# A two-layer hybrid trunk on one core: one product for the second token tile's scores, a reordered mLSTM block loop, one ScalarE table for its gates, and fewer early gate blocks

## The chip, the cores and the metric

The kernel runs on one core of one Trainium2 chip. The metric is the device time of one execution in microseconds (us). A core has five engines with a queue each: TensorE (PE in the profile, with its weight loads listed as PEld), VectorE (DVE), ScalarE (ACT), GpSimd (POOL) and SyncE (SP, which here only starts DMAs).

## The reference

Two layers over 256 tokens of width 1024, all in float32. Layer 0 mixes tokens with a gated MLP, layer 1 with an mLSTM block; after each mixer come a layer norm, a SwiGLU channel mixer, a second layer norm and a sigmoid-gated embedding. What the change touches is mostly the mLSTM mixer:

```python
xm, z = jnp.split(x @ w_in, 2, axis=-1)
xc = jax.nn.silu(causal_depthwise_conv(xm, conv_w, conv_b))
q = headwise_linear(xc, w_q)
k = headwise_linear(xc, w_k)
v = headwise_linear(xm, w_v)
gates = jnp.concatenate([q, k, v], axis=-1) @ w_gates + b_gates
...
s = jnp.einsum('bhtd,bhsd->bhts', qb, kb) * jnp.exp(dmat - m_t[..., None])
...
h = layer_norm(h, norm_g).reshape(B, S, ML_INNER) + skip * xc
return (h * jax.nn.silu(z)) @ w_out
```

and around it, in each layer:

```python
x = layer_norm(ALPHA * x + y, ln1_g[i], ln1_b[i])
x = layer_norm(ALPHA * x + swiglu(x, ffn_w_gate[i], ffn_w_up[i], ffn_w_down[i]), ln2_g[i], ln2_b[i])
gate = jax.nn.sigmoid(x @ ple_w_gate[i] + ple_b_gate[i])
x = x + gate * (p[i] @ ple_w_proj[i])
```

The chunk is 128 tokens, so the 256 tokens are two token tiles, and the gate recurrence is computed over the whole sequence at once.

## The kernel before, in words

**Numbers in two parts.** Every float32 operand of a product is split into a high part (a cast, on ScalarE) and a low part (the difference, on VectorE); the helper is `split` (L152 to L154). A product of two operands is then three products on TensorE: high by high, high by low, low by high. All these casts and subtractions carry L154 in the profile; the tile's name tells them apart (`w` for weights).

**Weights.** All weights arrive as 128 x 1024 blocks (512 KB) in one order, `weight_plan` (L76). `ahead(loads, casts)` (L171) starts loads up to `LOAD_AHEAD` blocks beyond the one in use and splits up to `casts` of them (usually four). A loaded block waits in one of four `raw` buffers; a buffer comes free when VectorE has written the block's low part, and SP then starts the next load. `EARLY` (L51) moves single blocks of the next stage forward in the order, behind named blocks: "mo" is the mLSTM output projection (16 blocks), "g" and "u" are the SwiGLU gate and up projections, "pj" the embedding projection, "pg" its gate, "z" the mLSTM's z projection, "xm" its other input projection. `behind["cast"]` names instructions; the split of a weight traced after that is queued behind them on their engine (L195), without waiting for their result. A layer norm sets it to its own last VectorE instruction (L346).

**The mLSTM block loop** (L799). For each of 16 feature blocks s: `xm_block(s)` (24 products of 256 columns, the causal convolution on VectorE, Silu, the split of xc, the skip term on GpSimd), `qv_block(s-2)` (q and v of an earlier block, with k folded into q, and 8 gate columns added to q and v each), `s_block(s-3)` (the scores). After the blocks named in `Z_AFTER_XM` (L45) comes one z block (24 products).

**The scores** (L777). Tile 0 of the keys meets all 256 tokens and the 8 gate columns: three products of 264 columns. Tile 1 meets only the second 128 tokens and the gate columns: three products of 136 columns. After the fourth block of a head, ScalarE copies scores and gate columns out of PSUM and GpSimd adds the gate columns to `gacc`.

**The gates** (L823 to L887). ScalarE's order there is the written one. z block 8 is multiplied with four transposes of `gacc` in it; then Exp, Ln and two scans on VectorE give the running gate values; z block 9; z block 10 with the transposes of the gate columns at step 3 (`transpose_cols`) and a broadcast of the gates for heads 0 and 1 at step 6; z block 11 with the broadcast for heads 2 and 3; per head three Exp, a product with the scores, a split. z block 12 and one Silu over five z blocks end this part. Then come four `pv_block`s with z blocks 13 to 15 between them.

**The end of the mLSTM and the boundary.** `Down` (L292) multiplies the output projection; for the last four blocks (`HOLD`) the second token tile's products are held back. `boundary` (L507) then runs the layer norm of tile 0 on VectorE while TensorE does the held products and the embedding projection, then the layer norm of tile 1 while TensorE goes on to `first(0)` (L524): for "g" and then for "u", 16 products with the high part of x that walk through the blocks 0 to 3 of the weight, then 8 with the low part. `rsqrt` (L317) is an addition and a power on GpSimd.

Of the kernel before, what the change touches and what calls it, by code (L numbers as in the profile page):

```python
# [11 lines left out]
AF = mybir.ActivationFunctionType  # L12
# [31 lines left out]
TOK = [slice(0, P), slice(P, 2 * P)]  # L44
Z_AFTER_XM = {3: 4, 7: 5, 11: 6, 15: 7}  # L45

# [4 lines left out]
EARLY = {("wo", 17 + k): ("g", 0, k) for k in range(4)}  # L51
EARLY |= {("mo", 6 + 2 * k): ("g", 1, k) for k in range(4)}
EARLY[("mo", 13)] = ("pj", 1, 0)
EARLY |= {("d", l, 10 + k): ("pg", l, k) for l in range(2) for k in range(6)}
# [80 lines left out]
def trunk(ctx, tc, a, out):  # L135
# [181 lines left out]
    def rsqrt(o, var, n=1):  # L317
        ve = tl("c", [P, 2], name="ve")
        pool.tensor_scalar(ve[:, :n], var, EPS, None, ALU.add)  # L319
        pool.tensor_tensor(o, ve[:, :n], mhalf[:, :n], ALU.pow)  # L320
# [177 lines left out]
    def channel_mixer(l, acc, last, hook=None):  # L498
# [8 lines left out]
        def boundary(j, g, b):  # L507

            w = weight("pj", l, j, casts=int(at["use"] <= place["pj", l, j]))
            ln_residual(0, acc.ps[0], g, b)  # L510
            acc.finish()
            project_p(j, w, 0)
            transpose_x(0)
            ln_residual(1, acc.ps[1], g, b)
            project_p(j, w, 1)
# [72 lines left out]
        def gate(t, pieces, before=(None, None)):  # L588
            ps = [bank("A", [P, c.stop - c.start], "gate") for c in pieces]
            if t == 0:  # L590
                gw.extend(None for _ in range(KD))
            for js in [[j] for j in range(len(pieces))] if t else [range(len(pieces))]:
                for i in range(2):
                    for k in range(KD):
                        if t == 0 and i == 0:
                            gw[k] = weight("pg", l, k)
                        if i == 1 and k == before[0]:
                            before[1]()
                        for j in js:
                            mm_part(ps[j], i, t, k, gw[k], pieces[j])  # L600
            return ps
# [20 lines left out]

        p0 = gate(0, HALF, (GATE_STEP, lambda: transpose_x(1)))
        embed(0, HALF, p0)
# [49 lines left out]
    def mlstm(embed1):  # L674
# [55 lines left out]
        def xm_block(f):  # L730
# [11 lines left out]
            for j in (1, 2, 3):  # L742
                dve.scalar_tensor_tensor(y[:, j:], ps[:, :S - j], par[:, f, 3 - j:4 - j], y[:, j:], ALU.mult, ALU.add)
            act.activation(y, y, AF.Silu)
            split(xm[1][:, 0, :], xm[1][:, 1, :], y)
            xms[f] = xm
            pool.tensor_scalar(a1[f // 8][:, f % 8, :], y, par[:, f, 5:6], None, ALU.mult)
# [29 lines left out]
        def s_block(f):  # L777


            h, j = f // 4, f % 4  # L780
            if j == 0:
                pss[:] = [bank("A", [P, S + 8], "s0"), bank("A", [P, GW], "s1")]
            q, k = qs.pop(f), xms.pop(f)[1]
            for s in range(2):
                m = slice(s * P, S + 8)
                pe.matmul(pss[s], k[:, 0, TOK[s]], q[:, 0, m], start=j == 0, stop=False)
                pe.matmul(pss[s], k[:, 0, TOK[s]], q[:, 1, m], start=False, stop=False)
                pe.matmul(pss[s], k[:, 1, TOK[s]], q[:, 0, m], start=False, stop=j == 3)
            if j == 3:
                t = tl("m2", [P, 384], name="sc")  # L790
                g = tl("cf", [P, 2, 8], name="gsum")
                act.copy(g[:, 0], pss[0][:, S:])
                act.copy(t[:, 0:S], pss[0][:, :S])
                act.copy(g[:, 1], pss[1][:, P:])
                act.copy(t[:, S:384], pss[1][:, :P])
                pool.tensor_tensor(gacc, gacc, g, ALU.add)
                sc.append(t)

        for s in range(NI + 3):  # L799
            if s < NI:  # L800
                xm_block(s)
            if s == 1:
# [3 lines left out]
            if 2 <= s < NI + 2:  # L806
                qv_block(s - 2)
            if s >= 3:
                s_block(s - 3)
# [259 lines left out]
```

## Time and profile before

| | us |
|---|---|
| median of 3 runs | 831.73 (830.5 to 832.65) |
| the profiled execution | 831.34 |
| its span, first to last instruction | 829.5 |

The granted TensorE clock was 0.999 of full speed over the span. The profile gives for each engine when each instruction started, how long it took, and what released it where it waited. A matmul's listed duration includes its way through the array; what counts for throughput is the distance from the start of one to the start of the next. In a row of the timeline the first number is the start (us from the start of the span), the second the duration, "x8" a count of merged instructions, and "[0.34 <-POOL q L760]" an idle time of 0.34 us that the named instruction ended.

### The profile page before, as it was taken

What the parts mean: (1) busy time and instruction counts of PE and PEld (TensorE: products, weight loads), DVE (VectorE), ACT (ScalarE), POOL (GpSimd) and SP (SyncE); (2) the same over time, 40 slices, a digit from 0 to 9 for tenths busy, and PEclk for the clock granted to TensorE, in tenths of its full rate; (3) what the DMA queues carried; (4) which work ended last, traced back from release to release, by engine and by line L of the source; (5) the groups of instructions that cost most, each with busy time, mean ns of one, the idle gap of its engine ahead of it and who ended that gap; (6) DMA issues with size and microseconds to landing.
All of it is one profiled execution on the core that took longest, in us unless ns stands there. A gap on an engine that the chain in (4) does not pass through costs nothing.

```text
span 829.5 us, 12434 instructions
## 1 busy us (share of the span) xinstructions
PE 820.4 (99%) x4536; PEld 710.5 (86%) x4536; DVE 615.1 (74%) x967; ACT 476.2 (57%) x825; POOL 157.0 (19%) x215
## 2 busy tenths in 40 slices
PE   9999999999999999999999999999999999999997
PEld 6888888888888888888889999898878888888886
DVE  7757998678945667586878988689885656776674
ACT  7555766566444546475347788776543555665522
POOL 1021633433100000700102766330010000000010
PEclk9999999999999999999999999999999999999999
DMA  8885456568286567586234444361746655776501
GB/s 303 293 310 176 152 171 212 181 202 275 98 282 198 171 208 251 165 289 199 67 135 148 141 142 157 123 237 55 253 139 242 202 179 188 262 242 220 178 1 52
DMA packets 44998, 155.54 MB, mean 188 GB/s; under 512 B 5256, under 2 KB 6024, under 8 KB 44936
## 3 DMA queue, kind: packets, MB, share of 16 engines
q1 hardware_dynamic: 44792, 154.60, 56.5%
q8 instruction: 36, 0.59, 0.3%
q10 hardware_dynamic: 144, 0.13, 0.1%
q14 instruction: 26, 0.21, 0.1%
HBM read 153.67 MB, written 1.05 MB: 187 GB/s over the span
## 4 chain that ended last, share of the span: by engine, by line
PE 83%; DVE 10%; DMA 3%; ACT 2%; POOL 1%; issue 1%; DVEq 0%; ACTq 0%; SPq 0%; POOLq 0%
PE pu L261 8%; PE pg L261 8%; PE acc L241 8%; PE acc L242 8%; PE acc L243 8%; PE ups L261 5%; PE pg L265 4%; PE pu L265 4%; DVE w L154 3%; PE ups L265 3%; PE vps L243 3%; PE vps L241 3%; PE vps L242 3%; PE first L287 2%; PE first L288 2%; PE first L290 2%
## 5 line engine op out<-in xcount | busy, mean ns | idle before, releaser
L154 DVE TENSOR_TENSOR w<-raw,w 128x1024 fp32r<-128x1024 f32 (+1 forms) x279 | 336.2, 1212 | 79.1 <-ACT w L154 77.9
L154 ACT CAST w<-raw 128x1024 fp32r<-128x1024 f32 (+1 forms) x278 | 286.7, 1041 | 129.0 <-PE acc L243 26.1
L241 PE MATMUL acc<-w,h 128*128 128x512 f32 x336 | 131.9, 393 | 0.3 <-ACT w L154 0.3
L243 PE MATMUL acc<-w,h 128*128 128x512 f32 x336 | 131.0, 390 | 1.1 <-DVE w L154 1.1
L242 PE MATMUL acc<-w,h 128*128 128x512 f32 x336 | 131.4, 391 | 0.0
L243 PEld LDWEIGHTS acc<-w,h 128*128 128x128 f32 x336 | 63.1, 188 | 15.5 <-DVE w L154 1.9
L241 PEld LDWEIGHTS acc<-w,h 128*128 128x128 f32 x336 | 63.2, 188 | 12.8 <-ACT w L154 1.1
L242 PEld LDWEIGHTS acc<-w,h 128*128 128x128 f32 x336 | 63.2, 188 | 10.9
L261 PE MATMUL pg<-xs,w 128*128 128x512 f32 x288 | 71.6, 391 | 0.0
L261 PE MATMUL pu<-xs,w 128*128 128x512 f32 x288 | 71.5, 390 | 0.0
L261 PEld LDWEIGHTS pu<-xs,w 128*128 128x128 f32 x288 | 53.8, 188 | 11.1
L261 PEld LDWEIGHTS pg<-xs,w 128*128 128x128 f32 x288 | 53.8, 188 | 11.0
L319 POOL TENSOR_SCALAR ve<-mv 128x1 f32<-128x1 f32 x8 | 6.1, 764 | 294.3 <-DVE mv L339 294.3
L272 ACT COPY s<-pg 128x256 f32<-128x256 f32 x36 | 13.4, 372 | 77.1 <-PE pg L265 77.1
L273 DVE TENSOR_TENSOR s<-s,pg 128x256 f32<-128x256 f32 x36 | 15.1, 420 | 48.8 <-ACT s L272 48.8
L261 PE MATMUL ups<-xs,w 128*128 128x512 f32 x192 | 47.7, 391 | 0.0
L261 PEld LDWEIGHTS ups<-xs,w 128*128 128x128 f32 x192 | 35.7, 188 | 7.2
L265 PEld LDWEIGHTS pg<-xs,w 128*128 128x128 f32 x288 | 38.9, 188 | 3.1
L265 PE MATMUL pg<-xs,w 128*128 128x256 f32 x288 | 39.5, 280 | 0.0
L265 PE MATMUL pu<-xs,w 128*128 128x256 f32 x288 | 39.4, 279 | 0.0
L241 PE MATMUL vps<-w,xs 128*128 128x512 f32 x96 | 37.5, 390 | 0.1
L242 PE MATMUL vps<-w,xs 128*128 128x512 f32 x96 | 37.5, 390 | 0.0
(242 smaller groups left out, 1639.9 us busy)
## 6 DMA issues: line engine op xcount, KB each, us to landing
raw<-in_ffn_g SPq DMA_DIRECT2D x44, 512.0 KB, 4.2
raw<-in_ffn_u SPq DMA_DIRECT2D x44, 512.0 KB, 4.2
raw<-in_ffn_d SPq DMA_DIRECT2D x44, 512.0 KB, 4.4
raw<-in_gm_u SPq DMA_DIRECT2D x24, 512.0 KB, 3.6
raw<-in_gm_wo SPq DMA_DIRECT2D x24, 512.0 KB, 3.5
raw<-in_gm_v SPq DMA_DIRECT2D x21, 512.0 KB, 4.8
raw<-in_ple_gate SPq DMA_DIRECT2D x16, 512.0 KB, 4.4
raw<-in_ml_z SPq DMA_DIRECT2D x16, 512.0 KB, 3.8
```

Of the source, the lines that this page charges most:

```text
L154: return dve.tensor_copy(hi, src) if fast else act.copy(hi, src), sub.tensor_tensor(lo, src, hi.bitcast(F32), ALU.subtract)
L241: pe.matmul(ps, lh, w[:, 0, c], start=start, stop=False)
L242: pe.matmul(ps, ll, w[:, 0, c], start=False, stop=False)
L243: pe.matmul(ps, lh, w[:, 1, c], start=False, stop=stop)
L261: pe.matmul(ps, w[:, 0, k * P:(k + 1) * P], xs[:, k], start=k == 0, stop=False)
L265: pe.matmul(ps[:, 0], w[:, 1, k * P:(k + 1) * P], xh[:, k, :], start=False, stop=k == KD - 1)
L272: act.copy(o, ps[:, 1])
L273: dve.tensor_tensor(o, o, ps[:, 0], ALU.add)
L287: pe.matmul(ps, xh[:, k, TOK[t]], w[:, 0, c], start=k == 0, stop=False)
L288: pe.matmul(ps, xh[:, k, TOK[t]], w[:, 1, c], start=False, stop=False)
L290: pe.matmul(ps, xl[:, k, TOK[t]], w[:, 0, c], start=False, stop=k == KD - 1)
L319: pool.tensor_scalar(ve[:, :n], var, EPS, None, ALU.add)
```

## The change

Seven edits, all in one step:

- `s_block`: for key tile 1, the high part of k meets both parts of q in one product of 2 x 136 columns into two halves of a bank, and the low part of k meets the high part of q in one of 136; the two halves are added on the way out (one ScalarE copy, one VectorE addition, and two GpSimd additions in place of one).
- `xm_block` is cut in two: Silu, the split of xc and the skip term become `xc_block(s)`, traced behind `qv_block(s-2)`.
- z blocks 4, 5, 6 follow blocks 1, 5, 10 in place of 3, 7, 11.
- In the gates' part: one table set with Exp and Ln is loaded ahead; `transpose_cols` stands at step 1 of z block 10, both broadcasts at steps 4 and 7 of it; z block 12 moves behind the first `pv_block`, and each of the four is followed by one z block.
- `EARLY`: three gate blocks (not four) come behind output blocks 8, 10, 12 (not 6, 8, 10, 12), and the embedding projection's first block is not moved any more.
- In the embedding's gate: two blocks (not four) are split ahead, and the next stage's first split is queued behind tile 1's transposes.
- `rsqrt`: the addition moves from GpSimd to VectorE.

```diff
-Z_AFTER_XM = {3: 4, 7: 5, 11: 6, 15: 7}
+Z_AFTER_XM = {1: 4, 5: 5, 10: 6, 15: 7}
...
-EARLY |= {("mo", 6 + 2 * k): ("g", 1, k) for k in range(4)}
-EARLY[("mo", 13)] = ("pj", 1, 0)
+EARLY |= {("mo", 8 + 2 * k): ("g", 1, k) for k in range(3)}
...
-        pool.tensor_scalar(ve[:, :n], var, EPS, None, ALU.add)
+        dve.tensor_scalar(ve[:, :n], var, EPS, None, ALU.add)
...
-            w = weight("pj", l, j, casts=int(at["use"] <= place["pj", l, j]))
+            w = weight("pj", l, j, casts=1)
...
-                            gw[k] = weight("pg", l, k)
+                            gw[k] = weight("pg", l, k, casts=min(2, KD - k))
...
-        p0 = gate(0, HALF, (GATE_STEP, lambda: transpose_x(1)))
+        def second_tile():
+            behind["cast"] = transpose_x(1)
+            ahead(LOAD_AHEAD, 1)
+        p0 = gate(0, HALF, (GATE_STEP, second_tile))
...
+            xms[f] = xm
+            return y
+
+        def xc_block(f, y):
             act.activation(y, y, AF.Silu)
-            split(xm[1][:, 0, :], xm[1][:, 1, :], y)
-            xms[f] = xm
+            split(xms[f][1][:, 0, :], xms[f][1][:, 1, :], y)
             pool.tensor_scalar(a1[f // 8][:, f % 8, :], y, par[:, f, 5:6], None, ALU.mult)
...
-                pss[:] = [bank("A", [P, S + 8], "s0"), bank("A", [P, GW], "s1")]
+                pss[:] = [bank("A", [P, S + 8], "s0"), bank("A", [P, 2, GW], "s1")]
...
-            for s in range(2):
-                m = slice(s * P, S + 8)
-                pe.matmul(pss[s], k[:, 0, TOK[s]], q[:, 0, m], start=j == 0, stop=False)
-                pe.matmul(pss[s], k[:, 0, TOK[s]], q[:, 1, m], start=False, stop=False)
-                pe.matmul(pss[s], k[:, 1, TOK[s]], q[:, 0, m], start=False, stop=j == 3)
+            s0, s1 = pss
+            pe.matmul(s0, k[:, 0, TOK[0]], q[:, 0], start=j == 0, stop=False)
+            pe.matmul(s0, k[:, 0, TOK[0]], q[:, 1], start=False, stop=False)
+            pe.matmul(s0, k[:, 1, TOK[0]], q[:, 0], start=False, stop=j == 3)
+            pe.matmul(s1, k[:, 0, TOK[1]], q[:, :, P:], start=j == 0, stop=False)
+            pe.matmul(s1[:, 0], k[:, 1, TOK[1]], q[:, 0, P:], start=False, stop=j == 3)
...
-                act.copy(g[:, 1], pss[1][:, P:])
-                act.copy(t[:, S:384], pss[1][:, :P])
-                pool.tensor_tensor(gacc, gacc, g, ALU.add)
+                act.copy(t[:, S:], s1[:, 1])
+                dve.tensor_tensor(t[:, S:], t[:, S:], s1[:, 0], ALU.add)
+                pool.tensor_tensor(gacc[:, 0], gacc[:, 0], g, ALU.add)
+                pool.tensor_tensor(gacc[:, 1], gacc[:, 1], t[:, 384:], ALU.add)
...
             if 2 <= s < NI + 2:
                 qv_block(s - 2)
+            if s < NI:
+                xc_block(s, y)
...
+            tc.keep_in_program_order(act.preload_act_table_set("natural_log_exp_and_others"))
...
-            z = z_mm(10, {3: transpose_cols, 6: broadcast_gates})
+            z = z_mm(10, {1: transpose_cols, 4: broadcast_gates, 7: broadcast_gates})
...
-                    z = z_mm(11, {2: broadcast_gates})
+                    z = z_mm(11)
...
-            z_copy(*z_mm(12))
-            act.activation(sz[1][:, 0:5, :], sz[1][:, 0:5, :], AF.Silu)
+            act.activation(sz[1][:, 0:4, :], sz[1][:, 0:4, :], AF.Silu)
...
-            if h < NH - 1:
-                z_act(*z_mm(13 + h))
+            z_act(*z_mm(12 + h))
```

More of the change, by code (lines that the diff above doesn't have):

```diff
@@ L781, in s_block @@
             if j == 0:
-                pss[:] = [bank("A", [P, S + 8], "s0"), bank("A", [P, GW], "s1")]
+                pss[:] = [bank("A", [P, S + 8], "s0"), bank("A", [P, 2, GW], "s1")]
             q, k = qs.pop(f), xms.pop(f)[1]
-            for s in range(2):
-                m = slice(s * P, S + 8)
-                pe.matmul(pss[s], k[:, 0, TOK[s]], q[:, 0, m], start=j == 0, stop=False)
-                pe.matmul(pss[s], k[:, 0, TOK[s]], q[:, 1, m], start=False, stop=False)
-                pe.matmul(pss[s], k[:, 1, TOK[s]], q[:, 0, m], start=False, stop=j == 3)
-            if j == 3:
[L790 to L793, printed above, removed]
-                act.copy(g[:, 1], pss[1][:, P:])
-                act.copy(t[:, S:384], pss[1][:, :P])
-                pool.tensor_tensor(gacc, gacc, g, ALU.add)
-                sc.append(t)
+            s0, s1 = pss
[4 more added lines that the diff above has]
+            pe.matmul(s1[:, 0], k[:, 1, TOK[1]], q[:, 0, P:], start=False, stop=j == 3)
+            if j == 3:
+                t = tl("m2", [P, 384 + 8], name="sc")
+                g = tl("cf", [P, 8], name="gsum")
+                act.copy(g, s0[:, S:])
+                act.copy(t[:, 0:S], s0[:, :S])
+                act.copy(t[:, S:], s1[:, 1])
+                dve.tensor_tensor(t[:, S:], t[:, S:], s1[:, 0], ALU.add)
+                pool.tensor_tensor(gacc[:, 0], gacc[:, 0], g, ALU.add)
+                pool.tensor_tensor(gacc[:, 1], gacc[:, 1], t[:, 384:], ALU.add)
+                sc.append(t[:, :384])
         for s in range(NI + 3):
             if s < NI:
-                xm_block(s)
+                y = xm_block(s)
             if s == 1:
```

## The prediction

> **What bounds the kernel now.** I read the page's first part first, then the busy times of the mLSTM's block loop (a window of 56 us), then TensorE's waits from the start of that loop to the end of the mLSTM.
>
> ```profile
> span 829.5 us, 12434 instructions
> PE 820.4 (99%) x4536; PEld 710.5 (86%) x4536; DVE 615.1 (74%) x967; ACT 476.2 (57%) x825; POOL 157.0 (19%) x215
> ```
>
> ```profile
> 464.00:520.00 56.00, 56.00 (x479) 56.00 (x479) 48.79 (x110) 44.74 (x121) 36.47 (x49) 1.00 0.46 151
> ```
>
> ```profile
> PEld acc L243 <- DVE w L154: 1.9, 2, 1.0
> PEld s L786 <- POOL q L760: 1.1, 2, 0.6
> PEld acc L241 <- ACT w L154: 1.1, 2, 0.8
> PEld vps L768 <- DVE q L154: 0.7, 1, 0.7
> PEld qps L247 <- DVE xm L154: 0.5, 1, 0.5
> PEld cp L850 <- DVE gt L840: 0.4, 1, 0.4
> ```
>
> TensorE is busy 99% of the span, and in the middle of the block loop (464 to 520) it never stands still, while VectorE works 48.79 of 56.00 us there. So an edit is worth what it takes off TensorE's own stream, plus the stalls in this short list that it ends, minus the stalls that it makes. Work taken off another engine is worth nothing by itself. All the stalls that the change can reach lie in five places: the start of the block loop (qps, and one of the two of "s"), its end (vps and the other "s"), the gates (cp), and the last output blocks (acc).
>
> **Part 1: the scores' products.** Here is one block of scores, with the v products ahead of it; what counts is the distance between starts.
>
> ```profile
> 516.42 0.29 PE L768 MATMUL vps<-w,xm 128*128 128x272 f32 x1
> 516.55 0.23 PE L769 MATMUL vps<-w,xm 128*128 128x136 f32 x1
> 516.61 0.34 PE L768 MATMUL vps<-w,xm 128*128 128x272 f32 x1
> ...
> 516.84 0.33 PE L786 MATMUL s<-q,xm 128*128 128x264 f32 x1
> 517.01 0.28 PE L787 MATMUL s<-q,xm 128*128 128x264 f32 x1
> 517.13 0.28 PE L788 MATMUL s<-q,xm 128*128 128x264 f32 x1
> 517.25 0.23 PE L786 MATMUL s<-q,xm 128*128 128x136 f32 x1
> 517.32 0.28 PE L787 MATMUL s<-q,xm 128*128 128x136 f32 x1
> 517.43 0.28 PE L788 MATMUL s<-q,xm 128*128 128x136 f32 x1
> 517.54 0.33 PE L246 MATMUL zps<-xs,w 128*128 128x256 f32 x1
> ```
>
> The six products take 517.54 - 516.84 = 0.70 us. A product of 136 columns holds the stream 0.07 us if a longer one stood before it (517.25 to 517.32), but 0.11 us in a row of short ones (517.32, 517.43, 517.54): then the next weight load isn't done. The pair that the change makes stands in the v products already: 272 columns take 0.13 us, the 136 behind them 0.06. The new block is 0.17 + 0.12 + 0.12 + 0.13 + 0.06 = 0.60 us, 0.10 less; 16 blocks give 1.6 us, all of it on TensorE's stream. The bounds are 0 (columns alone count) and 16 x 0.11 = 1.8 (one product in a row of short ones less).
>
> The Trainium skill, "TensorE: Matmul & The Clock Gate", section "Back-to-back issue gap", speaks against this part: its gap for an isolated product is the columns over 2.4 plus 2.5 ns, so that the same 408 columns for key tile 1 cost the same in two products as in three, but for one 2.5 ns; by it the part saves 16 x 2.5 ns = 0.04 us, an estimate. The rows disagree: 136 columns at 0.11 us are nearly twice that rule's 59 ns. For a stream of weight loads and products the same section gives about 81 ns at 128 columns, which is nearer and still below the rows.
>
> **Part 2: the block loop's stalls.** Four stalls, 0.5 + 0.7 + 1.1 = 2.3 us by weight loads. The qps stall is xc's low part arriving late for the first `qv_block`; z block 4 behind block 1 puts 24 products ahead of it. The other three have one cause: ScalarE, VectorE and GpSimd run in order, and Silu, xc's split and the skip term of block s stand ahead of q's split and the copy of q's gate columns (L760) of block s-2. `xc_block` behind `qv_block` turns that round. What is late next is xc, but it is wanted two blocks later, behind some 48 products. I take -2.3. The bound the other way is below, among the rivals: VectorE is 87% busy, gets four additions more, and z blocks now come after five blocks.
>
> **Part 3: the gates.**
>
> ```profile
> 528.51 1.28 ACT L835 ACT_TABLE_LOAD   x1
> ```
>
> ```profile
> L771 DVE TENSOR_TENSOR vsum<-vsum,vps 128x136 f32<-128x136 f32 x32 | 9.0, 284 | 0.3 <-ACT vsum L770 0.3
> ```
>
> The load in front of Ln stands in the chain from `gacc` to the transposes of the gate columns; without it the chain is 1.28 us shorter. The transposes come two steps earlier, 2 x 3 products of 0.12 us (517.01 to 517.13), 0.7 us. So 0.6 us of slack comes in for a wait of 0.4: -0.4. Against that, tile 1's gate columns now pass through one more VectorE addition (the L771 form, 0.28 us) and one more small GpSimd addition before z block 8's transposes at step 3, while TensorE gets there sooner: +0.3. Moving z block 12 changes no product; it brings the first `pv_block` forward by 24 products (2.8 us), which the shorter chain, the earlier broadcast and the missing table load in front of the third Exp pay back about; I take 0, with 0 to +0.8 as bounds.
>
> **Part 4: the output blocks and the gate blocks.** First what goes. In the last output blocks TensorE waits for splits:
>
> ```profile
> 600.93 0.39 PE L243 MATMUL acc<-w,h 128*128 128x512 f32 x1
> 601.65 0.50 PE L241 MATMUL acc<-w,h 128*128 128x512 f32 x1 [0.33 <-ACT w L154]
> 601.99 0.39 PE L242 MATMUL acc<-w,h 128*128 128x512 f32 x1
> 602.91 0.50 PE L243 MATMUL acc<-w,h 128*128 128x512 f32 x1 [0.53 <-DVE w L154]
> ```
>
> Undisturbed starts are 0.23 us apart (below), so these gaps of 0.72 and 0.92 us lose 0.5 and 0.7; the list above has the second kind twice, 1.9 us in all. Each block passes through one of four raw buffers, and before output block 15 the order held five foreign blocks; now it holds three, and the fourth gate block and the projection's block come after it. Two blocks less are two splits of about 1.2 us less ahead of blocks 14 and 15: -1.9, with 0 as the other bound.
>
> Then what comes. Here is the boundary behind it: VectorE, SP's loads, one ScalarE row, TensorE.
>
> ```profile
> 617.96 0.75 DVE L345 SCALAR_TENSOR_TENSOR xn<-xn,rs,row 128x512 f32<-128x512 f32 x1
> 618.63 4.62 DVE L154 TENSOR_TENSOR w<-raw,w 128x1024 fp32r<-128x1024 f32 x4
> ...
> 626.73 2.48 DVE L154 TENSOR_TENSOR w<-raw,w 128x1024 fp32r<-128x1024 f32 x2 [2.27 <-ACT w L154]
> ```
>
> ```profile
> 598.86 6.73 SPq L177 DMA_DIRECT2D raw<-in_ffn_u  x4
> ...
> 619.88 0.33 SPq L177 DMA_DIRECT2D raw<-in_ffn_g  x1
> ```
>
> ```profile
> 625.64 1.05 ACT L154 CAST w<-raw 128x1024 fp32r<-128x1024 f32 x1 [3.04 <-DMA raw<-in_ffn_g]
> ```
>
> ```profile
> 615.39 0.39 PE L287 MATMUL first<-w,xs 128*128 128x512 f32 x1
> 615.62 0.39 PE L288 MATMUL first<-w,xs 128*128 128x512 f32 x1
> ...
> 621.63 0.47 PE L287 MATMUL first<-w,xs 128*128 128x512 f32 x1
> ```
>
> Before, the four raw buffers hold the four up blocks through the two layer norms, and the four splits start when the second norm ends (L346 puts them behind it). Now the fourth gate block is first in that row, and the fourth up block has no buffer until that split is done. TensorE needs the gate block's low part at its 14th product, 615.39 + 13 x 0.23 = 618.4; the split, a quarter of the 4.62, ends at about 618.63 + 1.2 = 619.8: 1.4 us late. The fourth up block takes the place of the load that SP starts at 619.88, which ScalarE can cast at 625.64 and VectorE has split at 626.73 + 1.24 = 627.97. TensorE wants it at 621.63 + 13 x 0.23 = 624.6: 3.4 us late, which includes the first 1.4. All these times shift together with the end of the output products, so the gap stays. I take +3.4; the bounds are 1.4 (the up block comes in time after all) and 4.6 (one more split of 1.2 us ahead of the layer norm, by the embedding projection's block).
>
> **Part 5: what costs nothing.**
>
> ```profile
> L319 POOL TENSOR_SCALAR ve<-mv 128x1 f32<-128x1 f32 x8 | 6.1, 764 | 294.3 <-DVE mv L339 294.3
> ```
>
> `rsqrt`'s addition leaves GpSimd (0.76 us) for VectorE, in layer norms that run under held products; no wait of TensorE in the list, which covers one of the four boundaries, is on a layer norm. Without that cover it would be worth at most those 0.8 us per norm. Two gate blocks split ahead instead of four, with z's first split behind the transposes, clears ScalarE and VectorE in front of those transposes: a gain of at most a few tenths, taken as 0. ScalarE's missing table loads, other than Ln's, lie in its idle time.
>
> **The sum.** -1.6 - 2.3 - 0.4 + 0.3 - 1.9 + 3.4 = -2.5 us. The sum is made against the profiled execution's 831.34 us (span 829.5, 1.8 around it): 828.8 us. The median of the runs, 831.73, is 0.4 above that execution, well inside their spread. A measurement of this kernel can tell about 0.3%, 2.5 us, from no change, so the forecast stands on the edge of what counts as faster (829.2).
>
> **The rivals.**
> - *The late gate block does not bite* (VectorE gets its split in between the two layer norms, or the up block lands sooner): without +3.4 the sum is -5.9, 825.4 us. For it: layer 0's boundary shows no such stall; against it: there all four gate blocks were early, and L346 orders the splits. 0.22.
> - *The output blocks stay late too*, since their loads, not the number of blocks ahead, are what is slow (ScalarE waits there as well): +1.9, 830.7 us. 0.10.
> - *VectorE becomes the bound of the block loop; slower than before.* The place is blocks 1 to 15. It works 48.79 of 56.00 us; the rest is waiting that doesn't shrink if the order of its work is at fault. It decides as soon as those 7.2 us of idle time can't be cut by the 1.3 us that TensorE would gain there (some 13 blocks at 0.10). Then 1.6 and 2.3 are not gained, and four additions of 0.28 us come on top: +5.0 against the forecast, 833.8 us. For it: z blocks, which give VectorE time, now follow after five blocks; against it: no stall in the 56 us before. 0.08.
> - *No gain from the products*, by columns alone, as the page named in part 1 would have it: 828.8 + 1.6 = 830.4 us. The rows at 517.32 to 517.54 speak against it. 0.04.
> - *The forecast*: 0.52. Other mishaps, new waits in the gates above all: 0.04.
>
> **How the numbers follow.** Within the forecast's case, its unknown ends (1.4 or 4.6 for 3.4, 0.8 in the gates) spread it from about 826.9 to 830.8, a little more than half of it below 829.2: 0.31 faster, 0.21 same. The first rival adds 0.22 to faster; the second, the fourth and half of the third go to same, 0.18; the other half of the third, with most of the mishaps, makes 0.07 slower, and the last 0.01 is same. So 0.53, 0.40 and 0.07. The range reaches from the first rival's 825.4, a little lower for its own spread, to 832.0, which leaves out the third rival and little else.
>
> **What would show it.** Right: 32 products less, and 0.60 us from the first of a scores block to what follows; no wait at qps, vps, "s" or cp; no wait for weights in the output products; then a wait in `first` at the 14th product for the gate block's low part, and a second for the fourth up block, whose load starts only when the second layer norm is over; two ScalarE table loads less. Wrong: `first` runs without a wait (then 825.4), or waits appear inside the block loop on VectorE (then the third rival), or the stalls at blocks 14 and 15 are still there.

## The result, and the profile after

| | before | after |
|---|---|---|
| median of 4 runs each, us | 831.91 (830.5 to 832.65) | 827.16 (826.69 to 827.46) |
| the profiled execution, us | 831.34 | 827.14 |
| its span, us | 829.5 | 825.4 |

The ratio of the times is 0.9943, with a 95% interval of 0.9927 to 0.9959: 4.75 us less. The prediction was 828.8 us, 2.5 less than the profiled execution of before, with a range from a little under 825.4 to 832.0 and "faster" as the likeliest case; the profiled executions differ by 4.2 us, their spans by 4.1. In all that follows, stages are compared within profiled executions, all of which had a granted clock of 0.999 or 1.0; e2 below alone has runs at a lower one (its six longest, 0.994 to 0.997), so that its median says little.

First the page of after: its span, its engines, and the chain that ended last. (Line numbers of after are shifted: `split` is L153, the products are L240 to L247 and L286 to L289, the scores L791 to L796.)

```profile
span 825.4 us, 12401 instructions
...
PE 817.7 (99%) x4520; PEld 708.6 (86%) x4520; DVE 615.5 (75%) x981; ACT 471.4 (57%) x819; POOL 152.3 (18%) x209
...
PE 95%; DVE 2%; DMA 1%; ACT 1%; issue 0%; SPq 0%; POOL 0%; DVEq 0%; ACTq 0%
```

TensorE has 16 products less (4520 for 4536, one in each scores block; the 32 in the prediction's list of signs were a slip) and stays the bound; VectorE's busy time is the same. Then the waits of TensorE's weight loads, from the block loop to the boundary behind the mLSTM (in all, times, longest):

```profile
PEld first L286 <- ACT w L153: 1.6, 1, 1.6
PEld acc L240 <- ACT hn L943: 0.6, 1, 0.6
PEld first L287 <- DVE w L153: 0.3, 1, 0.3
PEld cp L863 <- DVE gt L853: 0.3, 1, 0.3
PEld gp L840 <- POOL sums L804: 0.2, 1, 0.2
PEld num L915 <- POOL plo L153: 0.2, 1, 0.2
PEld qps L245 <- DVE q L153: 0.2, 1, 0.2
```

Of before's list the waits at "s", vps, qps (for `xm`, near the loop's start) and in the output products (acc for `w`) are gone. The qps in this list is another one, for q at the loop's end (519.50). The one at cp is still there, at 0.3 for 0.4, and a new one in `first` is the largest. Small ones have come in the gates (gp, num), and the one in the first output blocks (acc for `hn`) has grown from 0.2 to 0.6.

Where the 4.1 us came from is read off the start of each stage's first product on TensorE. A difference that changes from one row to the next arose between them.

| first product of | before | after | difference |
|---|---|---|---|
| layer 0's first stage | 4.92 | 5.17 | +0.25 |
| layer 0's embedding gate | 405.53 | 406.06 | +0.53 |
| the block loop (xmps) | 441.24 | 441.45 | +0.21 |
| the transposes of `gacc` (gp) | 526.49 | 522.91 | -3.58 |
| the output projection | 563.68 | 560.08 | -3.60 |
| the embedding projection (pps) | 611.78 | 606.03 | -5.75 |
| `first` | 615.39 | 609.65 | -5.74 |
| layer 1's channel mixer (pg) | 638.43 | 634.36 | -4.07 |
| the last product of all | 824.89 | 820.81 | -4.08 |

So the block loop gave 3.79 us (-3.58 less +0.21), the gates 0.02, the output products 2.15, and `first` took back 1.67. The embedding gate of layer 0 gave 0.32. What comes before it was 0.53 later, and all of that arose in the first 72 us, in a stage that the change leaves as it is. The runs below are there 0.2 to 1.1 later than the one profile of before. I take it as spread; that it isn't the change was not shown.

The block of scores as the change makes it:

```profile
510.24 0.34 PE L791 MATMUL s<-q,xm 128*128 128x264 f32 x1
...
510.65 0.29 PE L795 MATMUL s<-q,xm 128*128 128x272 f32 x1
510.78 0.23 PE L796 MATMUL s<-q,xm 128*128 128x136 f32 x1
510.84 0.33 PE L245 MATMUL xmps<-xs,w 128*128 128x256 f32 x1
```

From its first start to what follows it takes 510.84 - 510.24 = 0.60 us, as worked out, and its last product, behind one of 272 columns, holds the stream 0.06 us. In the busy times by window, before (first fence) and after (second), the loop's middle shows no wait of TensorE although VectorE works 47.08 of 51.00 us instead of 44.00:

```profile
464.00:515.00 51.00, 51.00 (x437) 51.00 (x437) 44.00 (x99) 41.01 (x110) 32.84 (x43) 1.00 0.44 147
```

```profile
464.00:515.00 51.00, 51.00 (x435) 51.00 (x434) 47.08 (x107) 42.22 (x113) 37.92 (x50) 1.00 0.48 153
```

Now the boundary: TensorE's timeline in `first`, then VectorE's, SP's and ScalarE's of the same time.

```profile
612.63 1.03 PE L326 MATMUL tp<-ident,xn 128*128 128x128 f32 x8
613.42 0.48 PE L286 MATMUL first<-w,xs 128*128 128x512 f32 x1
613.73 0.50 PE L287 MATMUL first<-w,xs 128*128 128x512 f32 x1
...
619.31 0.39 PE L286 MATMUL first<-w,xs 128*128 128x512 f32 x1
620.84 0.50 PE L286 MATMUL first<-w,xs 128*128 128x512 f32 x1 [1.14 <-ACT w L153]
621.18 0.40 PE L287 MATMUL first<-w,xs 128*128 128x512 f32 x1
...
622.11 0.49 PE L287 MATMUL first<-w,xs 128*128 128x512 f32 x1
622.44 0.39 PE L286 MATMUL first<-w,xs 128*128 128x512 f32 x1
```

```profile
612.45 4.62 DVE L153 TENSOR_TENSOR w<-raw,w 128x1024 fp32r<-128x1024 f32 x4
...
620.82 3.77 DVE L153 TENSOR_TENSOR w<-raw,w 128x1024 fp32r<-128x1024 f32 x3 [2.54 <-ACT w L153]
```

```profile
613.70 0.33 SPq L176 DMA_DIRECT2D raw<-in_ffn_u  x1
```

```profile
619.75 1.04 ACT L153 CAST w<-raw 128x1024 fp32r<-128x1024 f32 x1 [2.58 <-DMA raw<-in_ffn_u]
```

The loads do what the prediction says. The fourth gate block is the first of the four splits at 612.45 and done a quarter of 4.62 later, at about 613.6; SP starts the fourth up block's load at 613.70; its cast runs at 619.75 and its split at 620.82. TensorE's order is not the one the prediction counted in. Eight transposes stand at 612.63, right after the 13th gate product, where the gate block's low part is not there yet: they fill the first wait, and only 0.2 us is lost at 613.42 and 613.73 (starts 0.31 and 0.34 apart for 0.23). In the up part, products of the other tile's gate stand in between, so that TensorE waits at 619.31 only for the late block's cast (1.53 us to the next start, 1.3 lost), and comes to its low part five products later, at 622.11, when the split is just done. With 0.1 each at 621.18 and 622.44 that makes 1.7 us. The rows don't name the tile, but the counts of the two lines do: seven products of the other tile's gate (1.6 us) stand ahead of the last of the up part's first 16. The 8 products behind those 16 start 13.24 us after the first of `first` (622.89), where in before it is 9.99 (625.38): the late block put the up part back by 3.25 us, and 1.6 of it was filled with products that had to be done anyway.

How late the block is differs between kernels that leave this stage as it is: `first` takes from 0.98 us (e2) to 1.87 (e11) more in them than in before. SP starts the load at the same distance from the first product of `first` in both (4.06 us); ScalarE's cast follows 5.35 us after that in e2 and 6.23 in e11.

### The profile page after: what moved, and what is told of

Its sections match the earlier page's. It is cut to its first block, busy times and chain, and to the rows that moved or that the text cites. A ratio compares the mean times of both kernels' runs of the same rounds, so it can differ in the third digit from the quotient of the medians.

```text
span 825.4 us, 12401 instructions
## 1 busy us (share of the span) xinstructions
PE 817.7 (99%) x4520; PEld 708.6 (86%) x4520; DVE 615.5 (75%) x981; ACT 471.4 (57%) x819; POOL 152.3 (18%) x209
## 4 chain that ended last, share of the span: by engine, by line
PE 95%; DVE 2%; DMA 1%; ACT 1%; issue 0%; SPq 0%; POOL 0%; DVEq 0%; ACTq 0%
PE acc L240 9%; PE acc L241 9%; PE acc L242 9%; PE pu L260 8%; PE pg L260 8%; PE ups L260 5%; PE pg L264 4%; PE pu L264 4%; PE ups L264 3%; PE vps L242 3%; PE vps L240 3%; PE vps L241 3%; PE xmps L245 2%; PE xmps L247 2%; PE xmps L246 2%; PE gate L289 2%
## 5 line engine op out<-in xcount | busy, mean ns | idle before, releaser
L153 DVE TENSOR_TENSOR w<-raw,w 128x1024 fp32r<-128x1024 f32 (+1 forms) x279 | 336.1, 1212 | 74.2 <-ACT w L153 72.9
L153 ACT CAST w<-raw 128x1024 fp32r<-128x1024 f32 (+1 forms) x278 | 286.6, 1042 | 118.9 <-PE acc L242 23.5
L240 PE MATMUL acc<-w,h 128*128 128x512 f32 x336 | 131.8, 392 | 0.2 <-ACT hn L943 0.2
L240 PEld LDWEIGHTS acc<-w,h 128*128 128x128 f32 x336 | 63.2, 188 | 12.3 <-ACT hn L943 0.6
L319 POOL TENSOR_TENSOR rs<-ve,mhalf 128x1 f32<-128x1 f32 x8 | 7.6, 956 | 297.3 <-DVE ve L318 292.8
L240 PE MATMUL vps<-w,xs 128*128 128x512 f32 x96 | 37.6, 392 | 0.5 <-DVE w L153 0.5
```

The source lines that it names most:

```text
L153: return dve.tensor_copy(hi, src) if fast else act.copy(hi, src), sub.tensor_tensor(lo, src, hi.bitcast(F32), ALU.subtract)
L240: pe.matmul(ps, lh, w[:, 0, c], start=start, stop=False)
```

## The experiments

Every kernel is after with one thing changed, but for e6 and e11, which join two of the other edits, and the last, which starts from e4. Medians are followed by lowest, highest and count; ratios are to the kernel before, with 95% intervals. The kernels were measured in three groups, each beside before, whose median was 831.4 to 831.5 there and 831.91 beside after; "over after" is a difference of medians, and one under about 0.5 us says nothing. "The loop" is the time from the first xmps to gp: 85.25 us before, 81.46 after.

### e1: the scores' products as before

```diff
-            pe.matmul(s1, k[:, 0, TOK[1]], q[:, :, P:], start=j == 0, stop=False)
-            pe.matmul(s1[:, 0], k[:, 1, TOK[1]], q[:, 0, P:], start=False, stop=j == 3)
+            for s in range(2):
+                m = slice(s * P, S + 8)
+                pe.matmul(pss[s], k[:, 0, TOK[s]], q[:, 0, m], start=j == 0, stop=False)
+                pe.matmul(pss[s], k[:, 0, TOK[s]], q[:, 1, m], start=False, stop=False)
+                pe.matmul(pss[s], k[:, 1, TOK[s]], q[:, 0, m], start=False, stop=j == 3)
...
-                act.copy(t[:, S:], s1[:, 1])
-                dve.tensor_tensor(t[:, S:], t[:, S:], s1[:, 0], ALU.add)
+                act.copy(g[:, 1], pss[1][:, P:])
+                act.copy(t[:, S:384], pss[1][:, :P])
```

> The changed kernel with the old scores block: six products, the old copies out. Theory (a short product is held up by the next weight load, so the merged product saves 0.10 us in each of 16 blocks, on TensorE's own stream): 1.6 us more than the changed kernel's 827.2, so 828.8, and the stretch from the first xm product to the gates' transposes longer by 1.6. Rival (only streamed columns count): 827.2, the same stretch within 0.2. If the four VectorE additions had cost something, the rival would come out below 827.2.

Measured: 828.59 (827.79 to 828.83, 5 runs), ratio 0.9966 (0.9953 to 0.9978), 1.4 us over after. The loop takes 82.90 us, 1.44 over after. The end of one of its scores blocks:

```profile
516.10 0.28 PE L793 MATMUL s<-q,xm 128*128 128x136 f32 x1
516.21 0.28 PE L794 MATMUL s<-q,xm 128*128 128x136 f32 x1
516.32 0.33 PE L245 MATMUL zps<-xs,w 128*128 128x256 f32 x1
```

No wait stands in this loop that after doesn't have, and after's of 0.2 at the last qps is missing: without that wait the saving would be 1.6, as predicted. The second and third product of 136 columns hold the stream 0.11 us each; after has in place of all three one of 272 (0.13) and one of 136 (0.06). So the saving is one weight load a block, 1.4 us in all, and it is on the path. Columns alone would have given nothing. (The profiled execution, the fastest of the five, is only 0.65 over after's: its layer 0 came 0.3 earlier and `first` lost 0.55 less.)

### e2: xc in its old place, the new places of the z blocks

```diff
-            return y
+            xc_block(f, y)
...
-                y = xm_block(s)
+                xm_block(s)
...
-            if s < NI:
-                xc_block(s, y)
```

> The changed kernel with Silu, xc's split and the skip term traced where they were, inside the xm block. Theory (they stand ahead of q's split and copy on in-order engines): the waits of the v products and of the scores at the loop's end come back, 1.2 us, and perhaps the 0.6 at its start: 828.4 to 829.0. Rival (z block 4 behind block 1 had cured the loop by itself): 827.2, no new wait.

Measured: 833.28 (831.33 to 837.41, 11 runs), ratio 1.0023 (1.0008 to 1.0037). The runs spread widely and the profiled execution is the fastest of them, so that its 4.2 us over after's (831.33 for 827.14) is the least that this costs. By it the kernel is level with before (831.33 for 831.34). The loop takes 86.00 us, 4.54 over after and 0.75 over before. TensorE's weight loads wait for GpSimd and VectorE:

```profile
PEld s L791 <- POOL q L766: 3.2, 4, 2.3
PEld vps L774 <- DVE q L153: 1.1, 3, 0.5
```

The longest of them on TensorE, what GpSimd does then, and what it does at that time in after:

```profile
465.02 0.39 PE L791 MATMUL s<-q,xm 128*128 128x264 f32 x1 [2.11 <-POOL q L766]
```

```profile
462.67 2.14 POOL L753 TENSOR_SCALAR a<-conv,par 128x256 f32<-128x256 f32 x1
464.77 0.47 POOL L766 CAST q<-wx 128x16 fp32r<-128x16 f32 x3
```

```profile
461.10 0.20 POOL L766 CAST q<-wx 128x16 fp32r<-128x16 f32 x1
...
462.46 2.14 POOL L753 TENSOR_SCALAR a<-conv,par 128x256 f32<-128x256 f32 x1
```

The copy of q's 8 gate columns takes 0.2 us, but it stands behind the skip term of a later block, 2.14 us long. In after the copy comes first. That the move of xc matters was expected; its size, 4.2 us or more, was not: the expected 1.2 to 1.8 were before's waits, but with the z blocks in their new places the same queue bites in four places of the loop (around 462.6, 484, 505 and 522).

### e11: xc and the z blocks as before

To tell the queue from the z blocks: e2's edit, and `Z_AFTER_XM` as before.

```diff
-Z_AFTER_XM = {1: 4, 5: 5, 10: 6, 15: 7}
+Z_AFTER_XM = {3: 4, 7: 5, 11: 6, 15: 7}
...
-                y = xm_block(s)
+                xm_block(s)
```

> The changed kernel with xc's part inside the xm block and z blocks 4 to 6 at their old places: of the block loop only the merged product is changed. Theory (the loop's four waits of 2.3 us come from the order of xc's part and z's places, the 4.3 us of waits with xc's part alone put back from the z blocks' absence where they had covered it): the four waits of the kernel before come back, 2.1 to 2.3 us, 829.3. Rival (the merged product alone makes new waits, or takes the old ones away): over 830 or under 828.5.

Measured: 829.81 (829.27 to 830.25, 10 runs), ratio 0.998 (0.9971 to 0.9989). The loop takes 83.79 us, 2.33 over after, and before's waits are back:

```profile
PEld s L791 <- POOL q L766: 1.5, 2, 1.2
PEld vps L774 <- DVE q L153: 0.5, 1, 0.5
PEld qps L246 <- DVE xm L153: 0.4, 1, 0.4
```

That is the 2.3 us of the prediction's part 2, by the waits that it named, though now most of it at one "s".

### e8: only the z blocks as before

```diff
-Z_AFTER_XM = {1: 4, 5: 5, 10: 6, 15: 7}
+Z_AFTER_XM = {3: 4, 7: 5, 11: 6, 15: 7}
```

> The changed kernel with z blocks 4, 5, 6 behind blocks 3, 7, 11 again. Theory (z block 4 behind block 1 is what gives xc its lead for the first q products): the wait of 0.5 us there comes back and no other: 827.7. Rival (with xc's part behind the q and v block the order of z blocks no longer matters): 827.2.

Measured: 827.93 (827.55 to 828.43, 5 runs), ratio 0.9959 (0.9945 to 0.9974). The loop takes 81.99 us, 0.53 over after, all of it at the first qps. So with xc moved, z block 4's new place pays 0.5; with z as before, xc's move pays 1.8 (e11 to e8). The two depend on each other: with xc in its old place the new z order costs 2.2 us more (e2 to e11).

### e9: no table set loaded ahead

```diff
-            tc.keep_in_program_order(act.preload_act_table_set("natural_log_exp_and_others"))
```

> The changed kernel without the table set loaded ahead: the sets are chosen at each function again. Theory (Ln's load stands in the chain from the gate sums to the transposes of the gate columns, which now come at step 1): 1.28 us more in that chain, a wait of 0.3 + 1.3 = 1.6 us there: 828.5. Rival (something else on TensorE covers it): 827.2.

Measured: 828.38 (827.82 to 828.89, 4 runs), ratio 0.996 (0.9945 to 0.9975), 1.2 over after; 1.8 in the spans. Its waits that after hasn't, or has shorter:

```profile
PEld acc L240 <- ACT hn L942: 0.8, 1, 0.8
PEld num L914 <- POOL plo L153: 0.8, 1, 0.8
PEld qps L245 <- DVE q L153: 0.5, 1, 0.5
```

The sum came out near the expected 1.3, the places didn't, and part of it by luck. From the gates to the first output blocks 1.0 us comes out, 0.2 of it at cp, 0.5 at num and 0.2 in the output blocks. Another 0.55 stands at the loop's end, ahead of any Exp or Ln, and `first` lost 0.16 more. The loop's end is a matter of order: in e9 the split of one more weight block stands ahead of the splits of xm and q there; after has none at that place.

```profile
518.07 1.20 DVE L153 TENSOR_TENSOR w<-raw,w 128x1024 fp32r<-128x1024 f32 x1
519.20 0.41 DVE L153 TENSOR_TENSOR xm<-conv,xm 128x256 fp32r<-128x256 f32 x1
```

So the two table loads that after saves here are worth some 1.0 us by this trace.

### e3: the early blocks as before

```diff
-EARLY |= {("mo", 8 + 2 * k): ("g", 1, k) for k in range(3)}
+EARLY |= {("mo", 6 + 2 * k): ("g", 1, k) for k in range(4)}
+EARLY[("mo", 13)] = ("pj", 1, 0)
...
-            w = weight("pj", l, j, casts=1)
+            w = weight("pj", l, j, casts=int(at["use"] <= place["pj", l, j]))
```

> The changed kernel with the old early blocks: four gate blocks behind output blocks 6, 8, 10, 12 and the projection's block behind 13. Theory by the two traces' stages (the output products won 2.1 us, the late gate block gave 1.7 back): 827.6. Rival, the sizes of the prediction (1.9 won, 3.4 given back): 825.7.

Measured: 825.62 (825.38 to 825.76, 5 runs), ratio 0.9931 (0.9918 to 0.9943), 1.5 *less* than after. `first` takes as long as before, and in the output products only 0.2 us comes back. So in this kernel the edit of `EARLY` is a loss, and something else cures the output products without it.

### e5 and e6: z block 12 ahead of the first pv block again

The suspect is z block 12, which with 13 to 15 now stands one place later, so that 24 products (2.8 us) more lie between the last `pv_block` and the output blocks. e5 moves it back; e6 moves it back and has e3's edit too.

```diff
-            act.activation(sz[1][:, 0:4, :], sz[1][:, 0:4, :], AF.Silu)
+            z_copy(*z_mm(12))
+            act.activation(sz[1][:, 0:5, :], sz[1][:, 0:5, :], AF.Silu)
...
-            z_act(*z_mm(12 + h))
+            if h < NH - 1:
+                z_act(*z_mm(13 + h))
```

> The changed kernel with z block 12 back in front of the first pv block, nothing between the last pv block and the output products. The old early blocks alone had brought back only 0.2 us of waiting in the output products, so what cured them is open. Theory A (z block 15 behind the last pv block gives the output blocks' splits 2.8 us more of a lead): waits of 1 to 2 us come back in the output products, 828.2 to 829.2. Theory B (two foreign blocks less ahead of block 15 are a cure of their own): no wait there, 827.2.

> The changed kernel with z block 12 back and the old early blocks: the output stage stands as in the kernel before. Theory A (the lead from z block 15): the 1.9 us of waits in the output products are back, no late gate block: 825.6 + 1.9 = 827.5. Theory B (the number of foreign blocks): the same 827.5, but then z12_back with the new early blocks has no such wait. Theory C (an earlier part of the change, the block loop or the gates, gave the lead): no wait, 825.6.

Measured: e5 826.75 (826.41 to 827.12, 4 runs), ratio 0.9949 (0.9934 to 0.9963); e6 826.70 (825.85 to 827.55, 4 runs), ratio 0.9948 (0.9933 to 0.9963). e5 has no wait for weights in its output products. In e6 they are back:

```profile
597.42 0.39 PE L243 MATMUL acc<-w,h 128*128 128x512 f32 x1
598.31 0.50 PE L241 MATMUL acc<-w,h 128*128 128x512 f32 x1 [0.50 <-ACT w L154]
598.65 0.39 PE L242 MATMUL acc<-w,h 128*128 128x512 f32 x1
599.57 0.50 PE L243 MATMUL acc<-w,h 128*128 128x512 f32 x1 [0.53 <-DVE w L154]
```

The gaps of 0.89 and 0.92 us, with one of 0.75 at 600.86, lose 1.9 us, as before's did. (Of e6's four runs the profiled one is the slowest, 827.55; its span is 1.8 over e3's, its median 1.1.) The four kernels make a square:

| | z block 12 ahead of the pv blocks | behind the first |
|---|---|---|
| `EARLY` as before | e6, 826.70: 1.9 us lost in the output products, none in `first` | e3, 825.62: 0.2 and none |
| `EARLY` of the change | e5, 826.75: none, and 1.7 in `first` | after, 827.16: none, and 1.7 |

Either edit ends the waits in the output products. With both, the second brings only its price. e5 and after can't be told apart by their times; by stage, e5 is 0.5 us shorter from the gates through the output blocks (0.15 up to the first of them, 0.36 behind it, where after waits for `hn`), and 0.4 of that is lost again by a later start of layer 0's embedding gate.

### e7: a buffer of its own for the fourth gate block

If the wait in `first` comes from the raw buffer, the fourth gate block in another buffer must end it, with the order as it is.

```diff
-            ap = plan[at["load"]][1]
+            key, ap = plan[at["load"]]
...
-            t = tl("raw", [P, n], name="raw")
+            t = tl("row" if key == ("g", 1, 3) else "raw", [P, n], name="raw")
```

> The changed kernel with the raw copy of the fourth gate block in a buffer of another tag (a row's), so that the four raw buffers hold all four up blocks through the layer norms. Theory (the fourth up block is late because its load has to wait for the fourth gate block's split): the wait of 1.1 us for a ScalarE cast in the first up products goes, 826.0; what the gate block's own split costs, 0.3 to 0.5, stays. Rival (the up block is late by VectorE's order, not by its load): 827.2.

Measured: 825.87 (825.3 to 826.03, 4 runs), ratio 0.9937 (0.9922 to 0.9951). SP now starts all four up blocks' loads ahead of the boundary, and at the place of the wait TensorE goes on:

```profile
592.45 4.16 SPq L176 DMA_DIRECT2D raw<-in_ffn_u  x4
```

```profile
613.00 1.03 PE L326 MATMUL tp<-ident,xn 128*128 128x128 f32 x8
...
619.24 0.61 PE L286 MATMUL first<-w,xs 128*128 128x512 f32 x2
```

`first` takes 0.13 us more than before, not 1.67. So the up block without a buffer is nearly the whole of the loss. The gate block's own late split costs next to nothing: the transposes cover it.

### e4: four early gate blocks, the embedding projection not moved

```diff
-EARLY |= {("mo", 8 + 2 * k): ("g", 1, k) for k in range(3)}
+EARLY |= {("mo", 6 + 2 * k): ("g", 1, k) for k in range(4)}
```

> The changed kernel with four gate blocks behind output blocks 6, 8, 10, 12, the projection's block left in its place. Theory (the fourth gate block's split and the fourth up block's load are what makes the first gate and up products late): those 1.7 us go and no wait is left in them; of the output products' 2.1 at most half comes back, as one foreign block less than in the kernel before stands ahead of block 15: 825.5 to 826.6. Rival (any fourth early block brings the whole wait in the output products back): 827.6.

Measured: 825.51 (825.32 to 825.71, 5 runs), ratio 0.993 (0.9917 to 0.9944). There is no wait in `first` and none for weights in the output products. It is the fastest of all, some 6 us under before and 1.65 under after, whose runs (826.69 to 827.46) don't overlap its own; e3 is not told apart from it.

### e10: the casts in the embedding's gate and rsqrt as before

```diff
-        dve.tensor_scalar(ve[:, :n], var, EPS, None, ALU.add)
+        pool.tensor_scalar(ve[:, :n], var, EPS, None, ALU.add)
...
-                            gw[k] = weight("pg", l, k, casts=min(2, KD - k))
+                            gw[k] = weight("pg", l, k, casts=None)
...
-        p0 = gate(0, HALF, (GATE_STEP, second_tile))
+        p0 = gate(0, HALF, (GATE_STEP, lambda: transpose_x(1)))
```

> The changed kernel with the embedding gate's splits four blocks ahead again, without the first z split behind the transposes, and with rsqrt's addition on GpSimd. Theory (the first of these freed ScalarE and VectorE in front of tile 1's transposes, the second is under cover): the stage from layer 0's embedding gate to z longer by 0.3 us, nothing elsewhere: 827.5. Rival (rsqrt is on the path of a layer norm): each of the boundaries longer by up to 0.5, 828.5 or more.

Measured: 828.24 (828.04 to 829.13, 4 runs), ratio 0.9963 (0.9949 to 0.9976), 1.1 over after. `first` takes 0.8 us more than in after, by both waits:

```profile
614.61 0.50 PE L287 MATMUL first<-w,xs 128*128 128x512 f32 x1 [0.41 <-DVE w L153]
...
621.96 0.73 PE L286 MATMUL first<-w,xs 128*128 128x512 f32 x2 [1.39 <-ACT w L153]
```

Of the 0.8, 0.45 is the norm's: `rsqrt`'s addition takes 0.69 us on GpSimd and 0.15 on VectorE, so that the norm ends later, and with it the split behind it and SP's load start 0.45 later (4.50 us after the first product of `first`, in place of 4.05). Another 0.24 is the load itself (6.29 us to the cast, in place of 6.05), which e2 and e11 show to differ without any edit here. Layer 0's embedding gate takes 0.09 us more. The rest of the 1.1 lies where no line of this edit runs: 0.26 in layer 0's down products (a wait for a weight's split at 353 us) and 0.32 in the loop (a longer wait at the last qps). So the part is worth at least 0.45 here, where zero was predicted, because the late gate block put the layer norm on the path; how much of the rest is chance was not tried, and the two edits were not tried apart.

### e12: e4, with the gates' transposes later

Two waits are left in the gates of e4: 0.2 at gp and 0.3 at cp. e12 gives both chains more time.

```diff
-            z8 = z_mm(8, {3: transpose_gates})
+            z8 = z_mm(8, {4: transpose_gates})
...
-            z = z_mm(10, {1: transpose_cols, 4: broadcast_gates, 7: broadcast_gates})
+            z = z_mm(10, {3: transpose_cols, 5: broadcast_gates, 7: broadcast_gates})
```

> The four early gate blocks behind output blocks 6, 8, 10, 12 (825.5), and the gates' transposes later: the first at step 4 of z block 8, the gate columns' at step 3 of z block 10, the broadcasts at 5 and 7. Theory (the waits left there, 0.2 and 0.3 us, are products too early by that much): both go, 825.0. Rival (the later broadcasts make the first pv block late): 825.5 or more, with a wait at its products.

Measured: 826.31 (825.94 to 826.9, 5 runs), ratio 0.9938 (0.9926 to 0.995), 0.8 over e4. Both waits are gone and stand further on:

```profile
PEld acc L240 <- ACT hn L943: 1.3, 1, 1.3
PEld num L915 <- POOL plo L153: 0.7, 1, 0.7
```

That fits a chain from the gates to the first output blocks which bounds this stage as a whole, wherever TensorE meets it first: given more time at cp, it costs more further on. In these two kernels the wait at cp was the cheaper.

## Why the prediction was right or wrong

**The bound.** Right. TensorE's stream and its few stalls carry every difference found; VectorE at 47.08 of 51.00 us made no wait in the loop's middle, so the third rival did not come about. A loop slower than before's did exist near it: with xc left in place, the new z order makes it 0.75 us longer (e2), with the longest wait behind GpSimd's queue and not by VectorE's load.

**Part 1, the products.** Right: 1.6 us predicted, 1.4 by e1 (1.6 but for a small new wait at the last qps), and 0.60 us from the block's start to what follows. The rule that the Trainium skill, "TensorE: Matmul & The Clock Gate", section "Back-to-back issue gap", gives for an isolated product, by which columns set the gap and the part would save next to nothing, does not hold in this stream: products of 136 columns stand 0.11 us apart in a row, 0.06 behind a longer one.

**Part 2, the loop's waits.** Right in size and cause: 2.3 predicted, 2.3 by e11. Together with part 1 the loop was to give 3.9 and gave 3.79. That xc's move carries 1.8 of it, and the z blocks 0.5, is e8 against e11.

**Part 3, the gates.** Right in the sum (-0.1, measured -0.02), wrong in its terms. The wait at cp did not go; it is 0.3. New waits stand at gp (the 0.2 of the predicted +0.3), at num and in the first output blocks. e9 shows that without the table loads some 1.0 us more comes out, along the whole chain and not at cp. z block 12's move, taken as 0 with bounds of 0 to +0.8, costs 0.5 by e5, most of it at the `hn` wait. That the sum still came out is in part luck.

**Part 4, the output blocks.** The size was right (1.9 predicted, 2.15 measured), the attribution only half. I credited it to the two foreign blocks fewer, and e5 shows that they do it alone; but the square of e3, e5 and e6 shows that z block 12's move does it as well, so that in this change they gave next to nothing. I had costed that move at nothing, and looked only at the gates ahead of it, not at the lead that it gives to the loads behind.

**Part 4, the late gate block.** This is the mis-sized term: +3.4 predicted, +1.67 measured, and nearly all of the gap between forecast and result. The buffer, the load and the split went as written, and e7 shows the cause. The step that failed is "TensorE wants it at" the 14th product: it took TensorE's order from the trace of before. In after the transposes stand ahead of the first late product, and products of the other tile between those of the late up block. The lateness itself was nearly right, 3.25 us; that 1.6 of it would be filled with seven products of the other tile was left out. A stall worked out in the old order was an upper bound here: the source of `first` is the same in both kernels, but the order in which TensorE gets its products isn't.

**Part 5.** Wrong in a way that the prediction half named. It called rsqrt's addition free under its cover, at most 0.8 us a norm without. The late gate block took the cover away at this boundary, where the norm's end came 0.45 us earlier for it (e10; the kernel as a whole 1.1, not all of it from this part). With e4's order, in which `first` has no wait, its worth was not tried. The 0.32 in layer 0's embedding gate, taken as 0 with a gain of a few tenths at most, is one wait for tile 1's x (at 417.5 in before); it is not back in e10, so that which edit ended it is open.

**The first rival** ("does not bite", 825.4) gives the time that e4 and e3 have. It was right on the sum of all the other terms, -5.9 (e4's span is 5.9 under before's), and wrong that the change would escape the late block.

So the forecast was 1.6 us too high, nearly all by one term. Two that it did not have, +0.53 in layer 0 ahead of the embedding gate and -0.32 in it, cancel in part, which is luck.

Left open: layer 0's first stage, 0.2 to 1.1 us later in these runs than in the one profile of before, and which edit ended the wait in layer 0's embedding gate.

## What to carry to other kernels

Count a product shorter than its weight load as a load, and look on the other in-order engines for small copies that stand behind a later block's long work: here the waits from that order, 2.3 us, cost TensorE more than the products saved. Before moving a block in a load order, ask which buffer it vacates and which load then has none, and whether another edit of the same change already gives the lead it is meant to give; try each without the other. A stall worked out in the old order of the engine that waits is a bound, not a forecast, if the order can come out otherwise.

## What the runs showed of the hardware

GpSimd's skip term, the same multiplication of 128x256 by a scalar per partition in all 16 blocks, took anything from 0.92 to 2.18 us in after; the subtractions of two such tiles took 0.73 to 0.75 in nearly all of the blocks. The groups of the two (busy, mean ns of one):

```profile
L753 POOL TENSOR_SCALAR a<-conv,par 128x256 f32<-128x256 f32 x16 | 22.8, 1427 | 8.9 <-ACT conv L751 8.9
L153 POOL TENSOR_TENSOR vn<-vsum,vn 128x256 fp32r<-128x256 f32 x16 | 12.4, 772 | 0.3 <-ACT vn L153 0.2 <-ACT gsum L800 0.2
```

A mean of 1.4 us hides the 2.14 that held up q's copy in e2. What VectorE does beside it goes with its length: beside the five that took 2.14 to 2.18 us in after, VectorE worked for 1.1 to 1.9 us on a weight block's split or on `bdm`; the nine that took 0.92 to 1.09 had neither beside them, and the two between (1.19 and 1.67) had 0.4 and 0.8 us of a split. The one in e2 has 1.1 us of `bdm` beside it. That one makes the other slow is not shown; no run changed it.

The load on which TensorE waits in after was cast 6.05 us after SP began to issue it (613.70 to 619.75), while ScalarE waited for it, and in the other kernels with the late block 5.35 (e2) to 6.29 us (e10); the median of that tensor's loads from issue to landing is 4.3 us:

```profile
raw<-in_ffn_u SPq DMA_DIRECT2D x44, 512.0 KB, 4.3
```
